# Spreading the factors of five norms over the partitions: two wide products of rounded parts in place of four plain fp32 products

## The chip, the cores and the metric

The kernel runs on one core of one Trainium2 chip. The metric is the device time of one execution in microseconds (us), median of three runs. The profile is one further execution of the same program; its times are those of that execution alone.

In the profile PE is TensorE's matmuls, PEld its weight loads, DVE is VectorE, ACT is ScalarE, POOL is GpSimd and SP the queue that issues most transfers.

## The reference

One layer of an encoder on 2048 tokens of width 1024, all fp32 (batch 1):

```python
mod = c_act @ w_ada[l] + b_ada[l]                       # sh1, sc1, gt1, sh2, sc2, gt2
h = rmsnorm(x, g_norm1[l]) * (1.0 + sc1) + sh1
proj = h @ w_in[l]                                      # 1024 x 3072: q, k, v of two head groups
# A: stick-breaking attention, 8 heads; B: chunked softmax attention with q/k norms, 8 heads
x = x + gt1 * (mixed @ w_o[l])
h = rmsnorm(x, g_norm2[l]) * (1.0 + sc2) + sh2
x = x + gt2 * (jnp.square(jax.nn.relu(h @ w1[l])) @ w2[l])
```

`rmsnorm(x, g)` is `x * rsqrt(mean(x*x, axis=-1) + EPS) * g`. The factor `rsqrt(...)` is one number for each token. There are two norms of the whole sequence, one ahead of each half of the layer.

## The kernel before

**Layout.** Activations stand transposed: the 128 partitions hold channels, the free axis holds 512 tokens (TB). The sequence is four such blocks, so there are eight norms of one block each: a3, a2, a1, a0 ahead of the projection, and m3, m2, m1, m0 ahead of the MLP. Since the tokens lie along the free axis, the factor of a token has to stand in every partition before VectorE can multiply by it.

**One norm.** ScalarE squares the eight tiles of a block and VectorE (GpSimd for m3 and m2) adds them to `acc`, 128 x 512. Four steps follow.

- `norm_columns` (L164): four fp32 matmuls with a column of ones add over the partitions; the sums come out as 128 x 4, one partition for each token of a group of 128.
- `norm_powers` (L170): VectorE scales them, GpSimd raises them to -1/2 with one Newton step (`rsqrt`, five instructions). The result `y` is 128 x 4.
- `norm_diagonal` (L178): VectorE makes four 128 x 128 diagonals `dg` (128 x 512 in all) from the identity and `y`.
- `norm_spread` (L191), or the same loop written out in `norm2`: for each of the four diagonals one fp32 matmul of 128 columns with a full square of ones. Each row of the result holds the factors of all 512 tokens.

`norm_rstd` (L185) calls the first three. In the profile these are the tiles `pva`/`pvm` (column sums), `nva`/`nvm`, `nya`/`nym`, `ndga`/`ndgm` (diagonals) and `pra`, `prm`, `psr` (the spread; `psr` is that of m1 and m0).

**Where the five norms stand.** The change touches a2, a1, a0 (`start_norm`, L455) and m1, m0 (`norm2`, L1304). a3 stands alone at the start, and m3, m2 run inside the attention stage by other functions (`finish_row`); both keep the plain form. In `start_norm` and `norm2` the steps are put between the matmuls of the main work by small counters (`norms`, `later`): `second` (sums, powers, diagonal) and, two or three banks of matmuls later, `third` (the spread and its use). TensorE, ScalarE, VectorE and GpSimd run strictly in this written order. The SP queue does so in the projection and the MLP; in the attention stage only part of its transfers are ordered.

**The main work** is done with operands split into a rounded part and a rest, both of type fp32r: three products of 128 x 512 for each product of the reference (`mm3`). The stages in order of time are the projection with the conditioning product `w_ada`, up to about 420 us; the attention of both groups, with the rest of the projection and the output projection as fillers between its matmuls, up to about 1320 us; then the last of the output projection and the MLP.

**Memory.** In the projection, results, value tiles and the parts of `w_o` leave through `stage` tiles (L330): pool `stp`, tag `st`, six buffers of 4096 bytes, taken in turn; a buffer is free again when its store to DRAM has landed. Pool `stp` holds the raw tiles `bg` (for `w_o` and the biases) as well. Pool `wp` (nine buffers `w`) holds the weight parts. Both lie behind pool `np_`, which holds the norms' small tiles: six tags (`nv`, `ny`, `nt`, `cv`, `cy`, `ct`) of two buffers, each in a slot of 32 bytes, 384 bytes in all, and a pad of 128 bytes (`padn`, L245) makes them 512. The first `st` buffer of the kernel before begins at byte 95,488 of each partition, which is 373 x 256. In the MLP the pool `accp` has twelve buffers of 2048 bytes (tag `c`), taken in turn by `kept` (L1290).

Of the kernel before, what the change touches and what calls it, by code (L numbers as in the profile page):

```python
# [9 lines left out]
F32 = mybir.dt.float32  # L10
F32R = mybir.dt.float32r
BF16 = mybir.dt.bfloat16
AF = mybir.ActivationFunctionType
ALU = mybir.AluOpType
# [4 lines left out]
P = 128  # L19
# [6 lines left out]
TB = 512  # L26
# [53 lines left out]
def encoder_kernel(ctx, tc, xT, c, g1, g2, w_in, w_rest, gqk, bias, w_o, w1, w2, w_ada, b_ada, out):  # L80
    nc = tc.nc
    act, dve, pool, sp = nc.scalar, nc.vector, nc.gpsimd, nc.sync
    pe = Ordered(tc, nc.tensor)
# [3 lines left out]
    cpool = ctx.enter_context(tc.tile_pool(name="cpool", bufs=1))  # L87
# [27 lines left out]
    ident = cpool.tile([P, P], F32, name="ident")  # L115
    make_identity(nc, ident)
    ones = cpool.tile([P, P], F32, name="ones")
    pool.memset(ones, 1.0)
    zero = cpool.tile([P, 1], F32, name="zero")
    pool.memset(zero, 0.0)  # L120
    mhalf = cpool.tile([P, 2 * NH], F32, name="mhalf")
# [29 lines left out]
    def norm_sums(pl, src, tg, eng=None, square=None):  # L151

        acc = pl.tile([P, TB], F32, tag="nsa", name=f"nsa{tg}")
        for k in range(KT):
            x = src(k)
            if k == 0:
                act.activation(acc, x, AF.Square)
                continue
            sq = square(k) if square else pl.tile([P, TB], F32, tag="nsq", name=f"nsq{tg}_{k}")
            act.activation(sq, x, AF.Square)  # L160
            (eng or dve).tensor_tensor(acc, acc, sq, op=ALU.add)
        return acc

    def norm_columns(pp, acc, tg):  # L164
        pv = pp.tile([P, TB], F32, tag="ps", name=f"pv{tg}")
        for i in range(4):
            pe.matmul(pv[:, i : i + 1], acc[:, i * P : (i + 1) * P], ones[:, 0:1], start=True, stop=True)
        return pv

    def norm_powers(pl, pv, tg):  # L170
        v = pl.tile([P, 4], F32, tag="nv", name=f"nv{tg}")
        dve.tensor_scalar(v, pv[:, 0:4], 1.0 / D, EPS, op0=ALU.mult, op1=ALU.add)
        y = pl.tile([P, 4], F32, tag="ny", name=f"ny{tg}")
        t = pl.tile([P, 4], F32, tag="nt", name=f"nt{tg}")
        rsqrt(y, v, t)
        return y

    def norm_diagonal(pl, y, tg):  # L178
        dg = pl.tile([P, 4, P], F32, tag="ndg", name=f"ndg{tg}", bufs=1)
        dve.tensor_tensor(  # L180
            dg, ident.unsqueeze(1).to_broadcast([P, 4, P]), y.unsqueeze(2).to_broadcast([P, 4, P]), op=ALU.mult
        )
        return dg

    def norm_rstd(pl, pp, acc, tg, meanwhile=None):  # L185
        y = norm_powers(pl, norm_columns(pp, acc, tg), tg)
        if meanwhile:
            meanwhile()
        return norm_diagonal(pl, y, tg)

    def norm_spread(pp, dg, tg):  # L191
        pr = pp.tile([P, TB], F32, tag="ps", name=f"pr{tg}")
        for i in range(4):
            pe.matmul(pr[:, i * P : (i + 1) * P], ones, dg[:, i, :], start=True, stop=True)
        return pr
# [43 lines left out]
    if True:  # L239
# [3 lines left out]
        np_ = pa.enter_context(tc.tile_pool(name="np_", bufs=2))  # L243
# [5 lines left out]
        pp, pq = Banks(zb), Banks(db)  # L249
# [80 lines left out]
        def stage(nm):  # L330
            return stp.tile([P, 2, TB], F32R, tag="st", name=f"st{nm}")
# [123 lines left out]
        def start_norm(tb, wait, more):  # L455
            tg = f"a{tb}"
            acc = norm_sums(np_, lambda k: xts[tb][k], tg)

            def second():
                dg = norm_rstd(np_, pq, acc, tg)  # L460

                def third():
                    r = norm_spread(pq, dg, tg)
                    for k, x in enumerate(xts[tb]):
                        dve.scalar_tensor_tensor(x, x, aff[:, 0, k : k + 1], r, op0=ALU.mult, op1=ALU.mult)

                norms.add(more, third)

            norms.add(wait, second)
# [18 lines left out]
        act, dve, pool = (Ordered(tc, e) for e in (act, dve, pool))  # L488
# [20 lines left out]
        for k in range(2):  # L509
            load_first(k)  # L510
        acc = norm_sums(
            np_, lambda k: xts[3][k], "a3",
            square=lambda k: stp.tile([P, TB], F32, tag="qh", name=f"nsqa3_{k}", bufs=6),
        )
# [15 lines left out]
        dg = np_.tile([P, 4, P], F32, tag="ndg", name="ndga3", bufs=1)  # L530
# [137 lines left out]
    if True:  # L668
# [522 lines left out]
        op = ph.enter_context(tc.tile_pool(name="op", bufs=2))  # L1191
# [14 lines left out]
        for i in range(len(steps) + LAG):  # L1206
# [29 lines left out]
            if i + 1 < len(steps):  # L1236
                u, st = steps[i + 1]
# [23 lines left out]
    if True:  # L1261
# [3 lines left out]
        accp = pm.enter_context(tc.tile_pool(name="accp", bufs=12, side="right"))  # L1265
        hop = {k: pm.enter_context(tc.tile_pool(name=f"hop{k}", bufs=1, side="right")) for k in range(2)}
        np2 = pm.enter_context(tc.tile_pool(name="np2", bufs=2, side="right"))
        pp = Banks(zb, zb, ab, db, zb, zb, ab, db)
# [18 lines left out]
        def temp(nm):  # L1287
            return tp.tile([P, TB], F32, tag="t", name=f"t{nm}")
# [4 lines left out]
        def bank(nm):  # L1293
            return pp.tile([P, TB], F32, tag="ps", name=f"ps{nm}")
# [3 lines left out]
        def at(n, job):  # L1298
            jobs.setdefault(n, []).append(job)
# [4 lines left out]
        def norm2(tb, step):  # L1304

            acc = rp.tile([P, TB], F32, tag="r", name=f"r{tb}")
            xs = {}

            def load(k):
                xs[k] = temp(f"xn{tb}_{k}")  # L1310
                sp.dma_start(xs[k], scr_x[tb, k])

            def add(k):
                x = xs.pop(k)
                act.activation(x if k else acc, x, AF.Square)
                if k:
                    dve.tensor_tensor(acc, acc, x, op=ALU.add)

            def second():
                dg = norm_rstd(np2, pp, acc, f"m{tb}")  # L1320

                def third():
                    pr = bank(f"r{tb}")
                    for i in range(4):
                        pe.matmul(pr[:, i * P : (i + 1) * P], ones, dg[:, i, :], start=True, stop=True)
                    dve.tensor_copy(acc, pr)
                    rows[tb] = acc

                later.add(2, third)

            for k in range(KT):
                at(step + k, lambda k=k: load(k))
                at(step + k + 4, lambda k=k: add(k))
            at(step + KT + 4, lambda: later.add(2, second))

        def right_blocks(mb, k, home):
# [307 lines left out]
        for mb in (1, 0):  # L1644
            begin = len(steps)
            steps += [First(mb, j, i) for j in range(NP) for i in PRODUCTS]
            for j in range(NP):
                f = steps[begin + 7 * j]
# [122 lines left out]
```

## Time and profile before

| | us |
|---|---|
| median of three runs | 2623.68 |
| the three runs | 2621.04, 2623.68, 2627.21 |
| the profiled execution, whole | 2628.16 |
| its span from first to last instruction | 2626.5 |
| PE busy | 2569.7 (98% of the span) |
| PEld busy | 2134.4 (81%) |
| DVE busy | 1885.4 (72%) |
| ACT busy | 1411.5 (54%) |
| POOL busy | 938.5 (36%) |
| TensorE's mean granted clock | 0.995 |

The busy times overlap. The program has 12,528 matmul records among 39,315 instructions. A duration in a row is that of one instruction from start to end; since matmuls overlap, what a matmul takes of TensorE is read from the start of one to the start of the next.

### The profile page before, as it was taken

What the parts mean: (1) busy time and instruction counts of PE and PEld (TensorE: products, weight loads), DVE (VectorE), ACT (ScalarE), POOL (GpSimd) and SP (SyncE); (2) the same over time, 40 slices, a digit from 0 to 9 for tenths busy, and PEclk for the clock granted to TensorE, in tenths of its full rate; (3) what the DMA queues carried; (4) which work ended last, traced back from release to release, by engine and by line L of the source; (5) the groups of instructions that cost most, each with busy time, mean ns of one, the idle gap of its engine ahead of it and who ended that gap; (6) DMA issues with size and microseconds to landing.
All of it is one profiled execution on the core that took longest, in us unless ns stands there. A gap on an engine that the chain in (4) does not pass through costs nothing. (4 is left out here: it accounts for less than half of the span.)

```text
span 2626.5 us, 39315 instructions
## 1 busy us (share of the span) xinstructions
PE 2569.7 (98%) x12528; PEld 2134.4 (81%) x12528; DVE 1885.4 (72%) x3233; ACT 1411.5 (54%) x2721; POOL 938.5 (36%) x1256
## 2 busy tenths in 40 slices
PE   7999999899999999999999999999999999999999
PEld 6888887778888888887888878788888888888887
DVE  7656765588789879998768787668766666555555
ACT  6333434777766686666754444466544444544443
POOL 4330244676666667776604323100002232200000
PEclk9999999999999999999999999999999999999999
DMA  9879889879976898756797777776765434375574
GB/s 348 327 292 370 314 308 292 252 243 296 317 231 219 251 275 262 249 189 196 224 336 247 254 248 269 264 288 224 265 216 175 161 141 168 125 256 194 199 270 154
DMA packets 257519, 650.68 MB, mean 248 GB/s; under 512 B 29472, under 2 KB 53024, under 8 KB 248224
## 3 DMA queue, kind: packets, MB, share of 16 engines
q1 hardware_dynamic: 256016, 643.45, 71.8%
q10 hardware_dynamic: 1296, 4.72, 0.4%
q8 instruction: 99, 1.62, 0.3%
q14 instruction: 108, 0.88, 0.1%
HBM read 456.69 MB, written 191.37 MB: 247 GB/s over the span
## 5 line engine op out<-in xcount | busy, mean ns | idle before, releaser
L42 PE MATMUL ps<-h,opw 128*128 128x512 f32 x2664 | 609.8, 391 | 5.4 <-DVE cx L42 3.9
L42 PE MATMUL ps<-oph,opv 128*128 128x512 f32 x2688 | 612.0, 389 | 0.1
L42 PEld LDWEIGHTS ps<-h,opw 128*128 128x128 f32 x2664 | 500.6, 188 | 114.0 <-DVE cx L42 6.4
L42 PEld LDWEIGHTS ps<-oph,opv 128*128 128x128 f32 x2688 | 504.2, 188 | 106.3 <-DVE opv L42 0.8
L42 ACT CAST wth<-wt 128x512 fp32r<-128x512 f32 (+3 forms) x544 | 257.2, 483 | 187.6 <-PE wt L42 176.0
L42 POOL TENSOR_TENSOR b<-p 128x512 f32<-128x512 f32 (+1 forms) x320 | 291.9, 912 | 177.4 <-DVE p L42 100.8
L42 DVE TENSOR_TENSOR wtl<-wt,wth 128x512 fp32r<-128x512 f32 (+3 forms) x544 | 290.5, 545 | 66.5 <-ACT wth L42 64.3
L42 DVE TENSOR_TENSOR oph<-hw,oph 128x512 fp32r<-128x512 f32 x224 | 156.5, 699 | 220.5 <-ACT oph L42 220.5
L42 ACT CAST oph<-hw 128x512 fp32r<-128x512 f32 x224 | 139.3, 622 | 283.4 <-PE ps L42 269.5
L42 PE MATMUL pt<-w,ht 128*128 128x512 f32 x1248 | 288.2, 391 | 0.0
L42 POOL TENSOR_TENSOR ts<-w 128x512 f32<-128x512 f32 x32 | 43.7, 1365 | 671.0 <-DMA w<-in_w_dram 373.0
L42 PEld LDWEIGHTS pt<-w,ht 128*128 128x128 f32 x1248 | 232.9, 188 | 47.7
L42 DVE TENSOR_TENSOR_SCAN p<-z,p,zero 128x512 f32<-128x512 f32 x192 | 245.7, 1280 | 31.5 <-ACT z L42 26.2
L42 PE MATMUL acc<-wth,v 128*128 128x512 f32 (+3 forms) x544 | 221.5, 411 | 1.3 <-DMA v<-scr_v 1.3
L42 PE MATMUL z<-k,q 128*128 128x512 f32 (+3 forms) x640 | 186.1, 372 | 14.5 <-DMA k<-scr_k 6.7
L42 ACT ACTIVATE z<-z 128x512 f32<-128x512 f32 (+1 forms) x320 | 166.4, 520 | 57.4 <-PE z L42 53.7
L42 DVE TENSOR_TENSOR opw<-w,opw 128x512 fp32r<-128x512 f32 x127 | 106.6, 841 | 113.2 <-ACT opw L42 113.1
L42 PE MATMUL acc<-wtl,v 128*128 128x512 f32 (+3 forms) x544 | 186.0, 348 | 0.0
L42 POOL TENSOR_TENSOR e<-e,cols 128x640 f32<-128x640 f32 (+4 forms) x128 | 142.8, 1120 | 96.7 <-DVE cols L42 50.7
L42 PE MATMUL wt<-ident,b 128*128 128x128 f32 x1088 | 172.2, 274 | 0.8 <-DVE p L42 0.2
L42 PEld LDWEIGHTS wt<-ident,b 128*128 128x128 f32 x1088 | 137.1, 141 | 42.0 <-DVE wtl L42 1.9
L42 PE MATMUL po<-fx,ow 128*128 128x512 f32 x576 | 161.9, 393 | 0.7 <-DMA ow<-scr_wo 0.7
(194 smaller groups left out, 4087.7 us busy)
## 6 DMA issues: line engine op xcount, KB each, us to landing
hw<-scr_hid SPq DMA_DIRECT2D x112, 512.0 KB, 3.9
k<-scr_k SPq DMA_DIRECT2D x272, 128.0 KB, 4.7
v<-scr_v SPq DMA_DIRECT2D x136, 256.0 KB, 4.3
q<-scr_q SPq DMA_DIRECT2D x128, 256.0 KB, 5.5
w<-in_w_dram SPq DMA_DIRECT2D x64, 512.0 KB, 5.2
hw<-scr_s SPq DMA_DIRECT2D x64, 512.0 KB, 4.6
wa<-in_w_ada_dram SPq DMA_DIRECT2D x48, 512.0 KB, 6.6
ow<-scr_wo SPq DMA_DIRECT2D x24, 1024.0 KB, 6.4
```

What stands on the lines that cost most here:

```text
L42: return lambda *x, **y: self.tc.keep_in_program_order(f(*x, **y))
```

## The change

`dg` becomes two 128 x 512 tiles of type fp32r in place of one fp32 tile. VectorE rounds `y` to fp32r (`yh`), subtracts to get the rest (`yl`), and makes a diagonal from each. Two matmuls of 512 columns with a square of ones of type fp32r add both up in one bank. The two tiles come from a `stage` buffer for a2, a1 and a0, and from two buffers of `accp` for m1 and m0. A square `ones_r` is filled once at the start by GpSimd. The pad `padn` is left as it is.

```diff
+    ones_r = cpool.tile([P, P], F32R, name="ones_r")
+    pool.tensor_copy(ones_r, ones)
...
-    def norm_rstd(pl, pp, acc, tg, meanwhile=None):
+    def norm_rstd(pl, pp, acc, tg, dg):
         y = norm_powers(pl, norm_columns(pp, acc, tg), tg)
-        if meanwhile:
-            meanwhile()
-        return norm_diagonal(pl, y, tg)
+        yh = pl.tile([P, 4], F32R, tag="nyh", name=f"nyh{tg}")
+        yl = pl.tile([P, 4], F32, tag="nyl", name=f"nyl{tg}")
+        dve.tensor_copy(yh, y)
+        dve.tensor_tensor(yl, y, yh.bitcast(F32), op=ALU.subtract)
+        for l, part in enumerate((yh.bitcast(F32), yl)):
+            dve.tensor_tensor(
+                dg[l].rearrange("p (i f) -> p i f", f=P), ident.unsqueeze(1).to_broadcast([P, 4, P]),
+                part.unsqueeze(2).to_broadcast([P, 4, P]), op=ALU.mult,
+            )
+        return dg
+
+    def norm_row(pr, dg):
+        for l in range(2):
+            pe.matmul(pr, ones_r, dg[l], start=l == 0, stop=l == 1)
+        return pr
...
             def second():
-                dg = norm_rstd(np_, pq, acc, tg)
+                st = stage(f"ndg{tg}")
+                dg = norm_rstd(np_, pq, acc, tg, [st[:, l, :] for l in range(2)])
                 def third():
-                    r = norm_spread(pq, dg, tg)
+                    r = norm_row(pq.tile([P, TB], F32, tag="ps", name=f"pr{tg}"), dg)
...
             def second():
-                dg = norm_rstd(np2, pp, acc, f"m{tb}")
+                dg = norm_rstd(np2, pp, acc, f"m{tb}", [
+                    accp.tile([P, TB], F32R, tag="c", name=f"ndgm{tb}_{l}") for l in range(2)
+                ])
                 def third():
-                    pr = bank(f"r{tb}")
-                    for i in range(4):
-                        pe.matmul(pr[:, i * P : (i + 1) * P], ones, dg[:, i, :], start=True, stop=True)
+                    pr = norm_row(bank(f"r{tb}"), dg)
                     dve.tensor_copy(acc, pr)
```

## The prediction

> **What bounds the kernel now.** I read the page first: busy times, the slices, the chain that ended last.
>
> ```profile
> PE 2569.7 (98%) x12528; PEld 2134.4 (81%) x12528; DVE 1885.4 (72%) x3233; ACT 1411.5 (54%) x2721; POOL 938.5 (36%) x1256
> ...
> PE   7999999899999999999999999999999999999999
> ...
> PE 34%; DVE 1%; ACT 0%; issue 0%; DVEq 0%
> ```
>
> TensorE is busy in every slice, and the chain consists of its matmuls. A share over the whole span may hide a stage with another limit, so the second view is the busy time by stage. The columns are the stretch, its length, then the busy time of each engine with its instructions, the clock, the DMA share and GB/s.
>
> ```profile
> 60.00:420.00 360.00, 359.88 (x1678) 299.93 (x1677) 232.53 (x404) 132.81 (x245) 97.44 (x198) 1.00 0.85 321
> 420.00:1320.00 900.00, 871.79 (x4980) 731.99 (x4978) 743.07 (x1501) 625.88 (x1335) 613.16 (x882) 0.99 0.80 247
> ...
> 1700.00:1780.00 80.00, 80.00 (x364) 66.52 (x363) 53.78 (x89) 47.61 (x86) 3.61 (x10) 0.98 0.79 296
> ```
>
> The norms a2, a1 and a0 lie in the first of these stretches (spreads at 79.5, 252.2 and 308.5 us), m1 and m0 in the last (1725.3 and 1749.0). In both TensorE has no idle time to speak of: 0.12 us of 360 and none of 80. So TensorE time that goes there should come off the end, and what is added to VectorE (65% and 67% busy there) costs only where a matmul waits for it. The DMA engines are at 0.85 in the projection, the one other resource near its end.
>
> **The change part by part.** *The spread on TensorE.* The next view is the order of time on PE around the spread of a2: start, length, then the group and its count. The row of 72 is the run of matmuls behind m1's.
>
> ```profile
> 79.52 1.06 PE L42 MATMUL pra<-ndga,ones 128*128 128x128 f32 x8
> 80.33 0.47 PE L42 MATMUL pt<-w,ht 128*128 128x512 f32 x1
> 80.64 0.39 PE L42 MATMUL pt<-w,ht 128*128 128x512 f32 x1
> ...
> 1725.33 1.05 PE L42 MATMUL psr<-ndgm,ones 128*128 128x128 f32 x8
> ...
> 1726.14 16.61 PE L42 MATMUL ps<-oph,opv 128*128 128x512 f32 x72
> ```
>
> Four fp32 products appear as eight records, two passes each. A wide product of the kind that the change uses takes (16.61 - 0.39) / 71 = 0.228 us from start to start. From the first pass of the spread to the second wide product behind it is 80.64 - 79.52 = 1.12 us, of which one wide product is 0.23; the spread therefore takes 0.90 us (0.81 to the next start, and 0.08 by which that next one runs long). Two wide products take 2 x 0.228 = 0.46. The gain is 0.44 us for each norm; counted to the next start alone it is 0.81 - 0.46 = 0.35. For five norms that is 2.2 us (1.8 by the narrower count). I take 2.2, since the long product behind the spread appears only behind fp32 passes.
>
> *The column sums* keep their four fp32 products and cost what they did.
>
> *VectorE.* Each norm adds a copy and a subtraction of 128 x 4 and a second diagonal. The nearest rows:
>
> ```profile
> L42 DVE TENSOR_SCALAR nva<-pva 128x4 f32<-128x4 f32 x4 | 0.6, 154 | 0.0
> L42 DVE TENSOR_TENSOR ndga<-ident,nya 128x512 f32<-128x512 f32 x3 | 2.1, 692 | 6.9 <-POOL nya L42 6.9
> ```
>
> That is 2 x 0.15 + 0.69 = 1.0 us for each norm; that the output is fp32r changes nothing (0.68 us for `oph`, in the next fence). It lies between the diagonal and its spread, so the question is how far apart these are:
>
> ```profile
> 72.59 0.69 DVE L42 TENSOR_TENSOR ndga<-ident,nya 128x512 f32<-128x512 f32 x1 [2.25 <-POOL nya L42]
> ...
> 240.38 0.69 DVE L42 TENSOR_TENSOR ndga<-ident,nya 128x512 f32<-128x512 f32 x1 [2.32 <-POOL nya L42]
> 252.18 1.05 PE L42 MATMUL pra<-ndga,ones 128*128 128x128 f32 x8
> ...
> 305.36 0.69 DVE L42 TENSOR_TENSOR ndga<-ident,nya 128x512 f32<-128x512 f32 x1 [2.31 <-POOL nya L42]
> 308.48 1.05 PE L42 MATMUL pra<-ndga,ones 128*128 128x128 f32 x8
> ...
> 1723.51 0.69 DVE L42 TENSOR_TENSOR ndgm<-ident,nym 128x512 f32<-128x512 f32 x1 [2.25 <-POOL nym L42]
> 1724.12 0.68 DVE L42 TENSOR_TENSOR oph<-hw,oph 128x512 fp32r<-128x512 f32 x1
> ...
> 1745.97 0.69 DVE L42 TENSOR_TENSOR ndgm<-ident,nym 128x512 f32<-128x512 f32 x1 [2.24 <-POOL nym L42]
> ...
> 1748.99 1.05 PE L42 MATMUL psr<-ndgm,ones 128*128 128x128 f32 x8
> ```
>
> The diagonal is done 6.2, 11.1, 2.4, 1.1 and 2.3 us ahead of its spread (start plus 0.69, against the spread's start). An added 1.0 us leaves 0.1 in the tightest, m1, and the second diagonal is only wanted by the second product, 0.23 later. I take zero and keep 0.3 us as the bound, for m1 alone.
>
> Behind the diagonal in VectorE's order wait the splits `oph` and `opv`, which come 1.0 us later. They feed matmuls from a ring of eight operands, two to a step of 12 x 0.228 = 2.7 us; ScalarE's wait for PE ahead of the next such operand (the next fence) tells that the ring is full, three steps ahead. Cover is some 5 us; without it each norm would cost its 1.0 us.
>
> ```profile
> 1725.53 0.62 ACT L42 CAST oph<-hw 128x512 fp32r<-128x512 f32 x1 [1.05 <-PE ps L42]
> ```
>
> *Buffers.* In `accp` the twelve buffers are taken in turn; four more takings shift m1's diagonals onto tiles of the 15th of 16 column pairs, whose stores left before the stage with the norms began. No cost. In `stp` the extra tile makes each later store tile reuse a buffer one taking sooner. The tightest place is a1:
>
> ```profile
> scr_v<-sv SPq DMA_DIRECT2D x20, 512.0 KB, 7.0
> ...
> 242.35 1.24 SPq L42 DMA_DIRECT2D scr_v<-sv  x2
> 247.84 0.37 ACT L42 CAST sv<-pt 128x256 fp32r<-128x256 f32 x1 [0.49 <-DVE sv L42]
> 248.10 4.27 ACT L42 CAST w<-wr 128x512 fp32r<-128x512 f32 x8
> ```
>
> The write at 247.84 will want the buffer of a store issued at 242.35; with the median landing of 7.0 us it waits until 249.4, 1.5 us, and the weight casts behind it on ScalarE with it. The next piece's matmuls begin at 253 (behind the spread at 252.18), over 2 us behind the first part even then. I take zero; a ScalarE stall of over 3 us here would reach TensorE.
>
> *At the start,* one GpSimd copy of 128 x 128 for `ones_r`: bounded by 0.2 us (the fill of `ones`) and 0.4 us (a product of this size on two tiles). GpSimd's next work there starts at 14.59 us, so it is hidden.
>
> ```profile
> L42 POOL TENSOR_TENSOR b<-p 128x128 f32<-128x128 f32 x32 | 12.8, 400 | 6.7 <-ACT wth L42 3.3 <-DVE p L42 1.0 <-DVE wtl L42 0.2
> L118 POOL MEMSET ones<- 128x128 f32 x1 | 0.2, 205 | 0.0
> 14.59 1.02 POOL L42 TENSOR_TENSOR nya<-nva,mhalf 128x4 f32<-128x4 f32 x1 [12.85 <-DVE nva L42]
> ```
>
> *Addresses.* This part doesn't show in the diff. `np_` gets two new tags of two slots of 32 bytes, 128 bytes, and `ones_r` adds 512 ahead of it. `padn` stays, so `stp` and `wp` move by 640 bytes, to 128 past a multiple of 256. Every transfer of the projection into or out of them moves with them. The transfers in that stretch, with count and size each:
>
> ```profile
> scr_k<-st SPq DMA_DIRECT2D x22, 512.0 KB, 4.4
> scr_q<-st SPq DMA_DIRECT2D x20, 512.0 KB, 7.9
> scr_wv<-w SPq DMA_DIRECT2D x16, 512.0 KB, 11.2
> scr_w<-w ACTq DMA_DIRECT2D x8, 512.0 KB, 9.8
> DMA packets 44101, 115.40 MB, mean 321 GB/s; under 512 B 3342, under 2 KB 17678, under 8 KB 41763
> ```
>
> With `scr_v`, `w_o` and its two parts (8 each of 512 KB) and the biases (16 of 320 KB) it is 110 x 512 KB + 5 MB, 63 MB of 115.4, or 0.54. No transfer of this trace begins at such an address, so its price is unknown. If a shifted packet takes a share x longer, the engines have 360 x 0.85 x 0.54 x = 165 x us more to do, against 360 x 0.15 = 54 us free. The lower end is zero and the matmuls hide it up to x = 0.33. The upper end is x = 1 (each packet done twice), 111 us beyond the cover. I take zero, since no row speaks for a price, and the cover is broad.
>
> [...]
>
> *The sum.* 2628.16 us of the profiled execution less 2.2 is 2626.0. That execution is 4.5 us over the median of the runs, so against the median I forecast 2623.68 - 2.2 = 2621.5 us, 0.08% less. A measurement of this kernel can tell about 0.2%, 5.2 us, from no change (the three runs span 6.2 us).
>
> **The rivals.** The first needs a row of the view of waits, for 60 to 330 us (total, times, longest):
>
> ```profile
> ACT st L42 <- DMA scr_k<-st: 2.8, 1, 2.8
> ```
>
> *Shifted transfers bound the projection (slower).* Place: 60 to 420 us; price 165 x - 54 us; it decides from x = 0.33, and from about x = 0.37 it outweighs the gain and the 5.2 us. For it speaks the DMA share of 0.85. Against it: between 60 and 330 us ScalarE's and VectorE's only wait of note for a transfer is one for a `st` buffer, which is the place that would feel it first. At x = 0.5 the time is 2621.5 + 28 = 2650.
>
> *The gain goes at the seam (no change).* The 1.3 us won before 420 could return as a wait for the first keys of the attention:
>
> ```profile
> 423.45 0.70 PE L42 MATMUL z<-k,q 128*128 128x512 f32 x2 [1.90 <-DMA k<-scr_k]
> 415.54 1.22 SPq L376 DMA_DIRECT2D scr_v<-sv  x2
> ```
>
> Then only m1 and m0 count: 2623.68 - 0.9 = 2622.8. Against it: the loads of the keys stand in SP's order behind the last value store, which waits for the last projection's matmuls, so they move forward with them.
>
> *The unordered transfers of the attention fall out otherwise.* Between 420 and 1320 TensorE idles 28 us, the longest wait being one for keys:
>
> ```profile
> PE cz L42 <- DMA k<-scr_k: 8.1, 3, 5.9
> PE z L42 <- DMA k<-scr_k: 6.7, 4, 3.0
> ```
>
> A single transfer moved in SP's order is worth up to 5.9 us either way: 2615.6 to 2627.4.
>
> *The wide products don't take the wide price,* say 0.45 us each as the four narrow ones' half: no gain, 2623.7. Nothing speaks for it: all fp32r products of this size run at 0.228.
>
> **How the numbers follow.** The forecast (a gain of 1.8 to 2.2, within 0.2%) gets 0.58. The seam and the wide products without gain 0.14, within 0.2% too. The moved transfer gets 0.17: 0.13 for a gain over 5.2 us, since it adds to the 2.2, and 0.04 for a loss over 5.2. The shifted transfers get 0.11, all slower. So faster 0.13, same 0.72, slower 0.15. The forecast's own range, with the runs' spread of 3 us to either side, is 2618 to 2625. The whole range takes in a moved transfer with that spread below (2615.6 - 3 = 2612) and shifted transfers up to x = 0.4 above (2621.5 + 12 = 2634).
>
> **What the changed profile would show.** `pra` and `psr` with two records of 512 columns for each changed norm, about 0.46 us from first start to the next group's (wrong if 0.8); PE without idle time in the two stretches; a copy, a subtraction and two diagonals on VectorE, done before the spread starts (wrong if PE shows a gap behind `ndgm`); the DMA share at 0.85 to 0.90 in the projection with median landings as above. It is wrong at large if the landings of `scr_q`, `scr_k`, `scr_v` grow by half and PE waits before 420 us, or if PE's idle time between 420 and 1320 us moves from 28 by over 5 us.

## The result and the profile after

| | median of its runs, us | lowest to highest | ratio to before, 95% interval |
|---|---|---|---|
| before (same session) | 2621.04 | 2617.52 to 2627.21 | |
| changed | 2637.85 | 2637.56 to 2639.47 | 1.0061, 1.0046 to 1.0076 |

The change costs 0.61%, 16 us. Forecast were 2621.5 us and no change that can be measured; the range ended at 2634.

The profiled execution of the changed kernel took 2639.47 us against 2628.16. The page's own lines, span, busy times and chain:

```profile
span 2637.7 us, 39259 instructions
...
PE 2578.2 (98%) x12498; PEld 2133.6 (81%) x12498; DVE 1888.7 (72%) x3248; ACT 1412.0 (54%) x2721; POOL 943.3 (36%) x1257
...
PE 32%; DVE 1%; DMA 1%; ACT 1%; issue 0%; SPq 0%; DVEq 0%
```

TensorE is busy 8.5 us longer although it has less to do. The same columns by stage as in the prediction:

```profile
60.00:420.00 360.00, 356.78 (x1600) 289.94 (x1599) 228.89 (x402) 128.08 (x233) 94.34 (x191) 1.00 0.83 310
420.00:1320.00 900.00, 870.71 (x4945) 730.49 (x4944) 740.98 (x1490) 619.83 (x1319) 609.83 (x882) 0.99 0.80 249
```

In the projection TensorE now idles 3.2 us where it idled 0.1. The granted clock is not the difference: its mean is 0.995 in both profiled executions. The work as a whole falls further behind than 3.2 us. The median lateness of VectorE's and ScalarE's instructions against the same instructions of before grows from 0.3 us near 60 us over 2.9 near 220 to 12 near 380, is 14.4 through the attention and 11.3 at the end. So most of the loss arises before 420 us. Part of it is a steady drift. The rest comes in two steps, which the lateness of TensorE's own matmuls shows: 1.4 us at 257 us of the changed profile and 4.3 at 305. The groups of the projection's matmuls (24 to 420 us) show the drift; the mean duration of one, in ns, stands behind the busy time. The rows of before come first, then those of the changed kernel.

```profile
L42 PE MATMUL pt<-w,ht 128*128 128x512 f32 x1248 | 288.2, 391 | 0.0
L42 PE MATMUL pq<-ht,w 128*128 128x512 f32 x240 | 55.9, 391 | 0.0
L42 PE MATMUL px<-ident,qh 128*128 128x128 f32 x128 | 16.8, 273 | 0.1
```

```profile
L42 PE MATMUL pt<-w,ht 128*128 128x512 f32 x1221 | 290.4, 397 | 1.6 <-ACT w L42 1.2 <-DVE w L42 0.5
L42 PE MATMUL pq<-ht,w 128*128 128x512 f32 x240 | 57.2, 396 | 0.0
L42 PE MATMUL px<-ident,qh 128*128 128x128 f32 x120 | 15.7, 273 | 0.0
```

Every product with a weight part `w` lasts 5 to 6 ns longer; the fp32 transposes last as long as before. The same from start to start, in one run of 72 products in each kernel (before, then changed):

```profile
235.71 16.63 PE L42 MATMUL pt<-w,ht 128*128 128x512 f32 x72
```

```profile
239.38 16.97 PE L42 MATMUL pt<-w,ht 128*128 128x512 f32 x72
```

(16.63 - 0.39) / 71 = 0.229 us against (16.97 - 0.40) / 71 = 0.233. Over all successive starts of the products on weight parts, the commonest step was 227 ns and the median is now 232; the mean goes from 228.3 to 233.7 (steps under 400 ns). The products on `wide`, which lies in another pool and whose products stand between those on the first weight parts `wfirst` in the same microseconds, keep 227, while `wfirst` has 232. What distinguishes them is the address of the operand: in the changed program `wfirst` begins 128 bytes past a multiple of 256 and `wide` on one. There are 1,248 + 240 + 48 = 1,536 products on the moved weight parts; at 5.4 ns each they make 8.3 us.

Both steps follow from one wait of ScalarE's, at 251 us. The rows of ScalarE and PE:

```profile
250.87 0.37 ACT L42 CAST sv<-pt 128x256 fp32r<-128x256 f32 x1 [3.43 <-PE pt L42]
256.19 0.61 PE L42 MATMUL pra<-stndga,ones_r 128*128 128x512 f32 x2
256.84 0.37 ACT L42 CAST sv<-pt 128x256 fp32r<-128x256 f32 x1 [5.60 <-PE pra L42]
257.11 4.26 ACT L42 CAST w<-wr 128x512 fp32r<-128x512 f32 x8
257.78 0.50 PE L42 MATMUL pt<-w,ht 128*128 128x512 f32 x1 [0.98 <-ACT w L42]
...
304.75 1.05 PE L42 MATMUL pva<-ones,nsaa 128*128 128x1 f32 x8 [1.58 <-DVE nsaa L42]
```

A value tile was given the buffer of a1's diagonals, so ScalarE waited 5.6 us for the spread to read them. The weight casts stood behind it, and the matmuls waited for the casts. At 305 us they waited again, for the sums of the next norm, whose tokens SP had loaded late as well (the last of them landed at 302.5 us, where it had been 292.2). Behind this second wait the granted clock (the third number from the end) was 0.50 for 3.4 us:

```profile
306.70:310.00 3.30, 3.27 (x8) 2.62 (x9) 3.30 (x6) 3.15 (x7) 0.00 (x0) 0.50 0.83 323
```

Successive products start 427 ns apart there in place of 232, which makes about 1.6 of the 4.3 us.

In the MLP the spread of m1 has a gap of its own:

```profile
1736.85 0.69 DVE L42 TENSOR_TENSOR ndgm<-ident,nylm 128x512 fp32r<-128x512 f32 x1
1736.99 1.10 PE L42 MATMUL psr<-ndgm,ones_r 128*128 128x512 f32 x2 [0.69 <-DVE ndgm L42]
```

### The profile page after: what moved, and what is told of

It reads as the page before. It is cut to its first block, busy times and chain, and to the rows that moved or that the text cites. A ratio compares the mean times of both kernels' runs of the same rounds, so it can differ in the third digit from the quotient of the medians.

```text
span 2637.7 us, 39259 instructions
## 1 busy us (share of the span) xinstructions
PE 2578.2 (98%) x12498; PEld 2133.6 (81%) x12498; DVE 1888.7 (72%) x3248; ACT 1412.0 (54%) x2721; POOL 943.3 (36%) x1257
## 5 line engine op out<-in xcount | busy, mean ns | idle before, releaser
L42 PE MATMUL pt<-w,ht 128*128 128x512 f32 x1248 | 296.9, 397 | 1.6 <-ACT w L42 1.2
```

The costliest lines, as they stand in the source:

```text
L42: return lambda *x, **y: self.tc.keep_in_program_order(f(*x, **y))
```

## The experiments

Three theories were set against each other. *Address:* a matmul takes longer when an operand doesn't begin at a multiple of 256 bytes. *Transfer:* the shifted transfers are slower, the forecast's rival. *Added work:* VectorE's additional instructions and the buffers cost it. Each ratio is to the kernel before, measured in the same session; the rows come from four sessions.

| kernel | ratio | 95% interval | median step of `pt` / `pq` on `w`, ns |
|---|---|---|---|
| changed | 1.0061 | 1.0046 to 1.0076 | 232 / 232 |
| e1_repad: changed, pools back on the grid | 1.0014 | 1.0006 to 1.0023 | 227 / 227 |
| e2_shift_only: before, both pools + 128 bytes | 1.0035 | 1.0023 to 1.0046 | 232 / 232 |
| e4_stp_only: before, stage pool alone + 128 | 1.0006 | 0.9995 to 1.0017 | 227 / 227 |
| e5_wp_only: before, weight parts alone + 128 | 1.0037 | 1.0024 to 1.0049 | 232 / 232 |
| e6_shift64: before, both + 64 | 1.0032 | 1.0020 to 1.0043 | 230 / 233 |
| e7_shift256: before, both + 256 | 0.9997 | 0.9987 to 1.0006 | 227 / 227 |
| e9_cpool512: before, all pools on the left + 512 | 1.0004 | 0.9994 to 1.0013 | 227 / 227 |
| e10_stage_plain: before, diagonals in a stage buffer | 1.0007 | 0.9997 to 1.0017 | 227 / 227 |
| e11_own_nopad: changed, own tiles, shifted pools | 1.0050 | 1.0036 to 1.0063 | 232 / 232 |
| e3_repad_own: changed, on the grid, own tiles | 1.0009 | 0.9999 to 1.0019 | 227 / 227 |
| e8_own_late: e3 with a later spread in the MLP | 1.0001 | 0.9992 to 1.0010 | 227 / 227 |
| e12_ident: e8 with the identity on the grid | 1.0002 | 0.9993 to 1.0010 | 227 / 227 |

**The pad taken back (e1_repad).** The new small tiles take the place of the pad.

```diff
-        padn = pa.enter_context(tc.tile_pool(name="padn", bufs=1))
-        padn.tile([P, 32], F32, tag="pad", name="padn")
```

> The changed kernel without the pad of 128 bytes behind the norms' small tiles, so that the pools for stage tiles and weight parts begin at a multiple of 256 bytes again. Address theory (a matmul with an operand off the multiples of 256 bytes takes 232 ns from start to start where it took 227; some 1,700 such matmuls make 9 us): their pitch is back at 227 ns, the time 9 to 12 us under the changed kernel, 2625 to 2629, where before is 2621 in the same session. Transfer theory (shifted transfers are slower): the time falls as well, but the pitch stays at 232. Added-work theory (VectorE's 1.0 us for each norm and the stage buffers cost it): the time stays at 2638, ratio 1.006.

The pitch is back at 227 and 0.47% of the 0.61% are gone. That speaks against the added work as the main cause. Address and transfer it tells apart only by the pitch.

**The shift without the change (e2_shift_only).**

```diff
-        padn.tile([P, 32], F32, tag="pad", name="padn")
+        padn.tile([P, 64], F32, tag="pad", name="padn")
```

> The kernel before with 128 bytes more of pad and nothing else. Address theory: matmuls on the weight parts go from 227 to 232 ns, those on the other pools stay, and the time rises by 9 to 10 us, ratio 1.0035 to 1.004. Transfer theory: the time rises by as much or more, with longer landings of the stage stores and gaps of the matmuls ahead of them, the pitch at 227. Added-work theory: no change, ratio 1.000.

128 bytes of pad cost 0.35% by themselves, 9.2 us, with no gap of PE before 420 us. The first expectation put the number of products too high: 1,536, not 1,700, make 8.3 us.

**One pool at a time (e4_stp_only, e5_wp_only).** Both add a second pad ahead of the weight parts; e4 has the larger first pad as well.

```diff
+        padw = pa.enter_context(tc.tile_pool(name="padw", bufs=1))
+        padw.tile([P, 32], F32, tag="pad", name="padw")
         wp = pa.enter_context(tc.tile_pool(name="wp", bufs=WT))
```

> The kernel before with only the stage pool (results, value tiles, raw biases and output weights) moved by 128 bytes; the weight parts are back on the multiples of 256 by a second pad. Nearly all shifted transfers stay shifted, no matmul operand but the 128 transposed tiles does. Address theory: pitch 227, time as before within 0.1%. Transfer theory: the whole loss of the shift, 9 us or more, ratio 1.0035 and up. Added-work theory: no change.

> The kernel before with only the weight parts' pool moved by 128 bytes; the stage pool stays on the multiples of 256, and of the transfers only the 24 stores of weight parts are shifted. Address theory: the whole loss of moving both pools, ratio 1.0035, pitch 232 ns on the weight parts and 227 on the others. Transfer theory: little, ratio 1.000 to 1.001, pitch 227.

The weight parts alone carry the whole loss; the stage pool, with nearly all of the shifted transfers, none that can be measured. Rows of e4_stp_only and then of e5_wp_only, as above:

```profile
L42 PE MATMUL pt<-w,ht 128*128 128x512 f32 x1248 | 288.3, 391 | 0.0
L42 PE MATMUL pq<-ht,w 128*128 128x512 f32 x240 | 56.0, 391 | 0.0
```

```profile
L42 PE MATMUL pt<-w,ht 128*128 128x512 f32 x1238 | 292.6, 396 | 0.0
L42 PE MATMUL pq<-ht,w 128*128 128x512 f32 x240 | 57.3, 396 | 0.0
```

In `pt` the part `w` is the moving operand, in `pq` the stationary one; both pay (232 ns against 227). The transfer theory falls.

**How coarse the grid is (e6_shift64, e7_shift256, e9_cpool512).** The first two are the one line of e2 with 48 and 96 floats in place of 64. e9 adds an unused square of 512 bytes among the constants.

> The kernel before with stage and weight pools moved by 64 bytes in place of 128. Address theory, if any start off a multiple of 256 bytes counts alike: pitch 232 ns, ratio 1.0035, as with 128 bytes. If the loss follows what lies beyond the last multiple of 128 or 64: pitch 227 for a 64-byte grid, over 232 for a 128-byte grid, up to twice the loss (ratio 1.007). Transfer theory: as with 128 bytes.

> The kernel before with stage and weight pools moved by 256 bytes. Address theory with a grid of 256 bytes: pitch 227, ratio 1.000 within 0.1%. If the grid is 512 bytes: pitch about 232, 1.0035. If any move costs: as with 128 bytes.

> The kernel before with one more square of 512 bytes among the constants, filled once by GpSimd, as the change adds; every pool on the left moves by 512 bytes and stays on multiples of 256. Address theory with a grid of 256 bytes: pitch 227, ratio 1.000 within 0.1%. If the changed kernel's rest of 0.1% comes from where the pools lie (a coarser grid, or other timing of the attention's transfers): 1.001 and over.

256 and 512 bytes cost nothing that can be measured, 64 bytes nearly as much as 128. Of the powers of two, only a grid of 256 bytes fits these four shifts. At 64 bytes the moving operand pays about half as much (mean step 231.1 ns against 233.7 at 128), the stationary one a little more (234.7 against 233.8). Rows of e6_shift64:

```profile
L42 PE MATMUL pt<-w,ht 128*128 128x512 f32 x1246 | 291.2, 394 | 0.0
L42 PE MATMUL pq<-ht,w 128*128 128x512 f32 x240 | 57.5, 396 | 0.0
```

**The stage buffer (e3_repad_own, e11_own_nopad, e10_stage_plain).** e3 and e11 give the two diagonals tiles of the norms' own pool, e3 on the grid and e11 with the shift; e10 is the kernel before with its plain diagonals in a stage buffer.

```diff
-                st = stage(f"ndg{tg}")
-                dg = norm_rstd(np_, pq, acc, tg, [st[:, l, :] for l in range(2)])
+                dg = norm_rstd(np_, pq, acc, tg, [
+                    np_.tile([P, TB], F32R, tag="ndg", name=f"ndg{tg}", bufs=1),
+                    np_.tile([P, TB], F32R, tag="nsa", name=f"ndh{tg}"),
+                ])
```

> The changed kernel with both pools back on multiples of 256 bytes and with the two diagonals of the first three norms in tiles of their own instead of a stage buffer. Address theory with the buffer wait beside it: no 5.6 us wait of ScalarE for the spread of the second norm, no gap of the matmuls near 258 us, 1 to 3 us less than with the pad alone, and 2 us less than before: ratio to before 0.999. If the stage buffer cost nothing, it equals the kernel with the pad alone. Added-work theory: 1.004 to 1.006.

> The changed kernel with its shifted pools left as they are, but the diagonals of a2, a1 and a0 in tiles of their own. Address theory: pitch 232 stays, ratio 1.0035 to 1.0045; what it lies under the changed kernel's 1.0061 is the buffer's share, 0.15 to 0.25% (4 to 6 us). If the buffer's share is given back at the seam: 1.0055 to 1.0065.

> The kernel before, plain products and addresses as they were, but with the plain diagonals of a2, a1 and a0 in a stage buffer. It isolates the buffer wait. Buffer theory: ScalarE waits some 5 us for the spread near 251 us as in the changed kernel, the matmuls gap near 253 and 299 us, 5 us late at 320 us, of which the seam to the attention gives back part: ratio 1.0005 to 1.002. If the stage buffer costs nothing by itself: 1.000, and no gap.

The mechanism is shown: e10 has the wait and the gap without any other part of the change, and e3 and e11, which have the change without the lent buffer, have neither.

```profile
251.56 1.05 PE L42 MATMUL pra<-stndga,ones 128*128 128x128 f32 x8
252.66 0.37 ACT L42 CAST sv<-pt 128x256 fp32r<-128x256 f32 x1 [5.92 <-PE pra L42]
253.60 0.50 PE L42 MATMUL pt<-w,ht 128*128 128x512 f32 x1 [0.98 <-ACT w L42]
```

Its price is not settled. In e10's profile TensorE's work is 1.7 us later behind the wait than ahead of it and 3.1 us later from 302 us on (expected were 5); by 460 us all of that has come back. This looks like the seam, but the waits for keys up to there add up to 5.6 us against 5.9. What differs is the granted clock. The kernel before had 0.50 for 6.8 us from its longest wait for keys there, and e10 kept 1.00. The row of before, and then that of e10, 3 us later:

```profile
450.00:456.80 6.80, 5.57 (x18) 4.83 (x19) 2.70 (x3) 1.64 (x3) 3.54 (x7) 0.50 1.03 341
```

```profile
453.00:459.80 6.80, 6.41 (x38) 5.61 (x39) 4.54 (x8) 4.06 (x10) 4.36 (x10) 1.00 1.05 359
```

Such stretches of half clock come and go between executions: ahead of the last microseconds they add up to 6.8 us in e7's profile, 13.6 in e10's, 27.2 in e1's, and 23.9 in both that of before and that of the changed kernel. So one profile against another can't price the buffer. In time e10 costs 0.07%, with an interval that includes none. e11 lies 0.11% under the changed kernel, and e3 0.05% under e1, both inside their intervals. In e3's profile TensorE's work gains 0.45 us on before at each of the three spreads (0.9 us ahead in front of the first, 2.2 behind the last).

**The wait of m1 (e8_own_late).** The spread in the MLP one step later:

```diff
-                later.add(2, third)
+                later.add(3, third)
```

> The changed kernel with its pools on multiples of 256 bytes, the first three norms' diagonals in tiles of their own, and the spread of m1 and m0 written one step of the MLP later (three ticks in place of two). If TensorE's wait for m1's diagonal (0.7 to 0.9 us) is what is left: no such gap, 1 us less than the same kernel with two ticks, ratio to before 0.999 to 1.0005. If the rest comes from the attention's transfers, it stays at 1.0009 within its interval.

In its profile no matmul waits for the diagonal; the medians of this kernel and of before, 2625.17 and 2624.62, can't be told apart. It is the best form of the change, and no faster than before. It is 0.08% under e3, measured in another session and with overlapping intervals, so the wait's price in time isn't shown either.

**The identity on the grid (e12_ident).** Three small constants are put ahead of it, 128 bytes together.

> The repaired changed kernel (pools on multiples of 256 bytes, own tiles, later spread) with the identity and the two squares of ones moved by 128 bytes, onto multiples of 256; they lay 128 past one in every kernel so far. If the address counts for the 1,776 fp32 transposes with the identity as it does for the fp32r products: their pitch falls from 108 to 109 ns by 2 to 5 ns, 4 to 9 us of TensorE's time, ratio 0.997 to 0.999. If it counts only for wide fp32r products (the transposes' other operand was shifted in the changed kernel and their pitch stayed at 109): 1.000, pitch as before.

Nothing: the transposes start 109 ns apart in both kernels (median), for the stick-breaking weights and for the softmax weights alike. The address counted for wide fp32r products (232 ns against 227) and did not for these narrow fp32 ones. Type and width differ at once, so which of them decides stays open.

## Why the prediction was wrong

**The step that failed is "Addresses".** It saw that the pools move by 640 bytes, to 128 past a multiple of 256, and then charged this to the transfers alone: "its price is unknown ... I take zero". But the moved pool `wp` is read by 1,536 matmuls as well, and that reader wasn't costed at all. There the bound resource itself got slower (232 ns in place of 227), so the cover that was counted (54 us of free DMA time) had nothing to do with it. The rival "shifted transfers bound the projection" had the right sign and the right place with the wrong mechanism; e4 and e5 separate them. What the profile of before could have offered was the count: 1,248 and 240 products of one group at 391 ns each, where 5 ns on each is 7 us.

On the transfers the zero was right. The landings stayed, as these two rows of the changed kernel against 7.9 and 11.2 show, and e4 is within 0.06% of before.

```profile
scr_q<-st SPq DMA_DIRECT2D x20, 512.0 KB, 7.1
scr_wv<-w SPq DMA_DIRECT2D x16, 512.0 KB, 11.0
```

The share x by which a shifted packet was to take longer shows in no run (the DMA share of the projection is 0.83 against 0.85); its upper end, each packet done twice, was the author's estimate. On the matmuls the start of an operand decided 5 ns of 227.

**"Buffers" failed too, in size.** It said that each later store tile reuses a buffer one taking sooner and that ScalarE would wait 1.5 us at most. The six buffers aren't taken in strict turn: the fourth taking after the diagonals (two parts of `w_o` and two value tiles) got theirs, and the wait was 5.6 us. The text's own threshold held: "a ScalarE stall of over 3 us here would reach TensorE", and it did, by 0.98 us at 258 and 1.58 at 305.

**"VectorE" failed in one norm.** The copy, the subtraction and the diagonals are as costed (0.17, 0.16 and 0.69 us each), but m1's spread waited 0.69 us where at most 0.3 was allowed. VectorE fetches the column sums behind other work, and it began that 3.8 us after TensorE's first product for them, where it had been 2.2. So the margin of 1.1 us didn't hold. It was a narrow one even without the change: in the eight profiles with the plain spread the fetch began 2.1 to 3.3 us after. In the six with the change it was 3.8 to 4.6; by what path the change delays it is not shown.

**The gain on TensorE was right.** a2's spread in the changed kernel takes 0.46 us from its first product to the next group's, as worked out, and e3 gains 1.3 us at the three spreads of the projection, as forecast. But 2.2 us are 0.08% of this kernel, and no run could tell that from nothing. Whether the seam, given as a rival, takes the gain back stays open, since the profiles differ there by where the stretches of low clock begin (450 and 488 us before; 436, 467 and 505 in the changed kernel).

The parts, with e8 (the change's own instructions and none of these three costs) at 1.0001: m1's wait 0.08% (e3 over e8), the shift 0.35% (e2), the buffer 0.05% (e1 over e3). Together that is 1.0049, inside the interval of the measured 1.0061 and 0.12% below it. Of these only the shift is clear of noise. The steps from e3 to e11 (0.41%) and on to the changed kernel (0.11%) lead to 1.0061 by construction and prove nothing about the sum. Whether the shift costs more beside the change than without it stays open, and so do the prices of the buffer and of m1's wait.

## What to carry to other kernels

A new small tile can move everything allocated behind it. Ask of every pool that moves who reads it, and begin with the engine that bounds the stage: a few nanoseconds on each of its instructions outweigh what is hidden elsewhere (here 5.4 ns on each of 1,536 products made 8.3 us, and the shifted transfers nothing that could be measured). A buffer lent from a busy ring to a tile with a late reader ties the ring's writers to that reader (here ScalarE waited 5.6 us), so look at who gets the buffer next, not only at who had it before.

## What the runs showed of the hardware

- A product of 128 x 512 in fp32r started 227 ns after the one before when its operands began at multiples of 256 bytes, and 232 when the moving or the stationary one began 128 bytes past (medians of the kernel before against the changed one, e2 and e5; the mean went from 228.3 to 233.7 in the changed one). 64 bytes past cost the moving operand about half of that (mean 231.1 in e6) and the stationary one 6 ns (234.7); 256 and 512 cost nothing that could be measured (227 in e7 and e9, ratios 0.9997 and 1.0004).
- fp32 transposes of 128 columns started 109 ns apart (median) in every case: with the identity 128 bytes past the grid (before, e8) or on it (e12), and with their other operand 128 bytes past (changed).
- The durations of weight loads didn't show the shift (median 188 ns in the kernel before and in the changed one); the matmuls' steps did. By what path the address costs time is not shown.
- Behind TensorE's wait of 1.58 us at 305 us the granted clock was 0.50 for 3.4 us, and 128 x 512 products started 427 ns apart, which made about 1.6 us more. Before had such a stretch of 6.8 us at its wait of 3.0 us for keys at 451 us, and none at the one of 1.9 us at 423. What sets them off is not shown.
